# An output projection whose second half is a block of seven products, with x and x2 in quarters of the columns

## The chip, the cores and the metric

The kernel runs on one core of a Trainium2 chip. The core has five engines with a queue of instructions each: TensorE (PE in the profile) multiplies matrices into the accumulation banks (PSUM), VectorE (DVE) and ScalarE (ACT) do elementwise work, GpSimd (POOL) does a little elementwise work and issues transfers, SyncE (SP) issues transfers. They run side by side and wait for each other through semaphores. Each queue is worked in order, so an instruction that waits holds up all that is behind it on its engine.

The metric is the time of one execution on the device in microseconds, the median over the runs.

## What is computed

One layer of a decoder for 512 tokens of width 2048, in float32. What matters here is its end:

```python
        g_a, g_b = jnp.split(jax.nn.sigmoid(merge_logits), 2, axis=-1)
        merged = g_a * (o_a @ w_up_a[l]) + g_b * (o_b @ w_up_b[l])
        x = x + merged @ w_out[l]
        x = x + jax.nn.sigmoid(x @ w_ple_gate[l]) * (p[l] @ w_ple[l])
    return rms_norm(x, final_g)
```

`w_out` and `w_ple_gate` are 2048 x 2048, `merged` and `x` are 512 x 2048. The sum `x + merged @ w_out` is called x2 in the kernel. Ahead of this lie one wide input projection, attention with 16 heads and a gated mixing within chunks of 128 tokens.

## The kernel before

**Arithmetic.** Every float32 operand of the large products is split into a high part (rounded by ACT, helper `high`, line 132) and a low part (the rest, by DVE, helper `low`, line 138). A product is three matmuls: high by high, high by low, low by high. Weights come from DRAM as raw tiles and are split on the way; activations are kept split and transposed, 128 channels on the partitions and 512 tokens along the row, as 16 row tiles in four parts of four (`act_h`, `act_l`; slots h0 to h3 and l0 to l3 of one pool).

**Jobs.** All large products are `Job`s, and `gemm` (line 279) is a generator that issues their matmuls in order. The main program draws on it with `fill(n)` (n units of three matmuls or so) and `finish(name)` (up to a job's end), and puts other work between. A plain job ("N") has 512 columns; in each of its 16 steps it takes one row tile of weights and issues twelve matmuls (four token tiles, three matmuls each) into four banks. Each step first splits weights two steps ahead (`split_to`), then takes some pieces off a list of background work (`pop`; `state["pops"]` pieces in a step).

A job of kind "S" has 1024 columns as a 2 x 2 block of half the channels by half the columns, and half the tokens by half the channels on the other side. Seven products stand for eight: 28 steps of twelve matmuls instead of 32. It wants four sums of the activations (S1 to S4), made by `sum_chunk` and `s4_chunk` in the background; four differences of weights, made by DVE in `sum_to` (line 231); and at the end of the products the banks are put together by `evac_quad` (products 1, 5 and 6 are saved by ACT; 3, 7 and 2 are added to them; 4 is taken as it is). The products run in the order 1 and 5, 6 and 3, 7, 2 and 4. S1 lies in `ob_h`, S2 in `ob_l`, S4 in a tile `s4`; S3 goes out to DRAM and comes back into half of the activations' own tiles once their old values are done with. In the kernel before, the jobs vn, zb, m0 to m3, ua0 and ua1 are of this kind.

**Order.** pl (input embeddings), attention's projections and attention, u0, u1 (plain), vn, zb, m0 to m3 (seven products), ua0, ua1 (seven products), ub0 to ub3 (plain), wo0 to wo3 (plain, `w_out`), pg0 to pg3 (plain, `w_ple_gate`), and the tail with the norm and the stores. The order on each queue is written out by hand in the main program.

**Around the change.** After ub3, `turn_merged` has put the merged activations into the 16 row tiles. x is then loaded whole into the tile x2 (line 1448, four loads on POOL's queue). When a job wo ends, DVE adds its banks to x2's columns (line 667); six units later PE transposes the new quarter of x2 (line 1471, two turns of eight transposes), and ACT and DVE split it: the first half of the channels into `ob_h` and `ob_l`, the second into two more tiles, `ob2`. The gate jobs pg read those tiles. At their ends `evac_ple_gate` and `evac_last` use x2, the `ple` quarters (computed at the start and put into DRAM) and `final_g`.

Of the kernel before, what the change touches and what calls it, by code (L numbers as in the profile page):

```python
# [21 lines left out]
P = 128  # L22
# [15 lines left out]
class Job:  # L38
# [24 lines left out]
def kernel(ctx: ExitStack, tc: tile.TileContext, x, p, norm_g, w_in,  # L63
# [23 lines left out]
    small = const.tile([P, 80], F32, name="small")  # L87
# [5 lines left out]
    ph_act = ExitStack()  # L93
    edge = ctx.enter_context(tc.tile_pool(name="edge", bufs=1, side="right"))
    edge.tile([P, 56], F32, name="pad_r")
    actp = ph_act.enter_context(tc.tile_pool(name="actp", bufs=1, side="right"))
# [7 lines left out]
    for q in range(4):  # L104
        for i in "hl":
            new_part(i, q)

# [11 lines left out]
    ob_h = acts.tile([P, 8, S], F32R, name="ob_h")  # L119
    ob_l = acts.tile([P, 8, S], F32R, name="ob_l")  # L120
# [49 lines left out]
    def add_job(job):  # L170
        jobs.append(job)
        if job.kind == "S":
            half, c2 = job.kt // 2, job.c0 + job.cols
# [65 lines left out]
    def split_to(i, more=1):  # L239
        while state["high"] < len(subs):  # L240
            h = state["high"]
            job, k, n, ld = subs[h]
            if h > (i if job.kind == "S" else i + more):
                break
            sum_to(h)
            if job.kind == "S":
                hi = quad["pool"].tile([P, 2, job.cols], F32R, tag="hs", name="hs", bufs=3)
            elif k >= job.kt - job.tail:
                hi = f_tiles["th"][:, k - job.kt + job.tail:][:, :n]
            else:  # L250
                hi = stream.tile([P, n, job.cols], F32R, tag="hi", name="hi", bufs=4)
            src = source(h)
            high(hi, src)
            parts[h] = [hi, None, src]
            state["high"] += 1
        sum_to(i + 1)
        while state["low"] <= min(i, len(subs) - 1):
            job, k, n, ld = subs[state["low"]]
            pt = parts[state["low"]]
            if job.kind == "S":  # L260
                pt[1] = quad["pool"].tile([P, 2, job.cols], F32R, tag="ls", name="ls", bufs=3)
            elif k >= job.kt - job.tail:
                pt[1] = f_tiles["tl"][:, k - job.kt + job.tail:][:, :n]
            else:
                pt[1] = stream.tile([P, n, job.cols], F32R, tag="lo", name="lo")
# [186 lines left out]
    xs, ys = ("g", "g", "s", "s"), ("t", "t", "o", "o")  # L452
    vs_b, vw_b = ("t", "t", "s", "s"), ("o", "o", "t", "t")
# [84 lines left out]
    def part_act(p, k, t):  # L538
# [8 lines left out]
        o = {"5": ob_h, "6": ob_l}[p] if p in "56" else quad["s4"]  # L547
        return o[:, k, sl], o[:, k, t * P + 256:t * P + 256 + P]

    def evac_quad(final, place=None):  # L550
# [4 lines left out]
        def e(p, ps):  # L555
# [14 lines left out]
            else:  # L570
                for t in range(2):
# [3 lines left out]
                    final(2 + t, 0, stream.tile([P, 512], F32, tag="hi", name="c21", bufs=4), ps[t])  # L575
# [23 lines left out]

    ob2 = {}  # L600
# [29 lines left out]
    def load_gate_b(cg):  # L630
        up_tiles[cg] = up_tiles["pool"].tile([P, TT, 512], F32, tag="gate", name="gate", bufs=3)
        nc.gpsimd.dma_start(up_tiles[cg], gate_columns(1, cg))
# [29 lines left out]

    def evac_out(cg):
        def e(ps):
            for t in range(TT):
                sl = x2[:, t, 512 * cg:512 * cg + 512]
                nc.vector.tensor_tensor(out=sl, in0=sl, in1=ps[t], op=ALU.add)
# [5 lines left out]
    def x2_act(k):  # L673
        return ob_act(k) if k < 8 else (ob2["h"][:, k - 8], ob2["l"][:, k - 8])
# [28 lines left out]
    def evac_last(ps, t):  # L703
        ss, fg = f_tiles["ss"], f_tiles["fg"]
        if t == 0:
            f_tiles["rs"] = f_tiles["pool"].tile([P, TT, 2], F32, name="rs", bufs=1)
# [482 lines left out]
    def sum_chunk(c):  # L1189
# [16 lines left out]
        def s1():  # L1206
            op(None, l22, ALU.add)
            split(ob_h[:, k1, lo_t], ob_h[:, k1, hi_t], w["t"])

        def s2():  # L1210
            op(None, h11, ALU.subtract)
            op(None, l11, ALU.subtract)
            high(ob_l[:, k1, lo_t], w["t"])

        def s2_low():
            low(ob_l[:, k1, lo_t], ob_l[:, k1, hi_t], w["t"])
# [17 lines left out]
    def s4_chunk(c):  # L1234
# [4 lines left out]
        def first():  # L1239
            t = w["t"] = quad["pool"].tile([P, 2, 256], F32, tag="s1", name="sum", bufs=2)  # L1240
            h12, l12, h, l = (a.bitcast(F32) for a in (act_h(k2, lo_t), act_l(k2, lo_t),
                                                       ob_l[:, k1, lo_t], ob_l[:, k1, hi_t]))
# [4 lines left out]
        def second():  # L1247
            split(quad["s4"][:, k1, lo_t], quad["s4"][:, k1, hi_t], w["t"])
# [28 lines left out]
    ph_s4 = ExitStack()  # L1277
    quad["s4"] = ph_s4.enter_context(tc.tile_pool(name="s4p", bufs=1, side="right")).tile([P, 8, S], F32R, name="s4")
# [4 lines left out]
    for q in range(2):  # L1283
        for i, a in enumerate((act_h, act_l)):
            nc.gpsimd.dma_start(a(slice(4 * q, 4 * q + 4), slice(256, 512)), s3_dram[:, i, 4 * q:4 * q + 4])
# [86 lines left out]
    def load_oa(i, t):  # L1372
        t = t.rearrange("p a s -> p (a s)").rearrange("p (o h k s) -> p o h k s", h=2, k=4, s=256)
        n = t.shape[1]
        nc.gpsimd.dma_start(t, oa_dram[:, i:i + n])
        oa_slot.update((p, t[:, j]) for j, p in enumerate("1563724"[i:i + n]))

    load_oa(0, ob_h)
    fill(4 * 8)
    load_oa(2, ob_l)  # L1380
    load_oa(4, quad["s4"])
# [3 lines left out]
    ph_7 = ExitStack()  # L1385
    load_oa(6, ph_7.enter_context(tc.tile_pool(name="oa7", bufs=1)).tile([P, 4, S], F32R, name="oa7"))
# [13 lines left out]
    ph_7.close()  # L1400
    ph_q.close()
    ph_s4.close()


    obp = ctx.enter_context(tc.tile_pool(name="obp", bufs=1))
    fp = ctx.enter_context(tc.tile_pool(name="fp", bufs=1))
    f_tiles["ss"] = fp.tile([P, TT, 4], F32, name="ss")
    for i in "hl":
        ob2[i] = obp.tile([P, 8, S], F32R, name="ob2" + i)
    ph_up = ExitStack()  # L1410
    up_tiles["pool"] = ph_up.enter_context(tc.tile_pool(name="gatep", bufs=1))
# [31 lines left out]
    state["pops"] = 2  # L1443
    ph_up.close()
    mp = ctx.enter_context(tc.tile_pool(name="mp", bufs=1))
    x2 = mp.tile([P, TT, D], F32, name="x2")
    for t in range(TT):
        nc.gpsimd.dma_start(x2[:, t], x[t * P:t * P + P])


    free_banks = {0: "to", 1: "gs", 2: "to", 3: "gs"}
    for cg in range(4):
        finish(f"wo{cg}")
        if cg == 3:
            ph_act.close()
            fq = f_tiles["pool"] = ctx.enter_context(tc.tile_pool(name="fq", bufs=2))
            fg = f_tiles["fg"] = fq.tile([P, D], F32, name="fg", bufs=1)
            nc.gpsimd.dma_start(fg, bass.AP(tensor=final_g.tensor, offset=final_g.offset, ap=[[0, P], [1, D]]))
            for i in range(4):
                ple_t[i] = fq.tile([P, TT, 512], F32, tag="ple", name="ple", bufs=4)  # L1460
                nc.gpsimd.dma_start(ple_t[i], spilled(i))
            f_tiles["th"] = fq.tile([P, 8, 512], F32R, name="th", bufs=1)
            f_tiles["tl"] = fq.tile([P, 8, 512], F32R, name="tl", bufs=1)
            state["pops"] = 1
        fill(6)
        for j in (0, 2):
            pair = [bank(free_banks[cg][i], "ps_x2") for i in range(2)]
            for i, b in enumerate(pair):
                for t in range(TT):
                    k = 4 * cg + j + i  # L1470
                    nc.tensor.transpose(b[:, t * P:t * P + P], x2[:, t, k * P:k * P + P], ident)
            for i, b in enumerate(pair):
                h, l = x2_act(4 * cg + j + i)
                split(h, l, b)
            fill(8 if cg < 3 else 16)
# [26 lines left out]
```

## Time and profile before

| | |
|---|---|
| median of 3 runs | 1585.43 us |
| lowest and highest | 1585.24 and 1585.61 us |
| profiled execution | 1584.71 us |
| its span, first to last instruction | 1583.0 us |
| mean granted clock of TensorE | 0.999 |

The span is what the profile's views divide up; the profiled execution's time has 1.7 us around it. In the page, a line such as `L138 DVE ... lo<-raw,hi` is a group of instructions: line of the kernel, engine, operation, tile written from tiles read, sizes, count, busy time in all and mean of one, then the idle time of the engine just before them and what ended it. Matmuls overlap on TensorE, so that their mean durations add up to more than the time that passes.

### The profile page before, as it was taken

To read this page: it belongs to the slowest core of one execution; us is meant where nothing else is said; L and a number is where in the kernel's file an instruction comes from. 1 tells how busy PE (TensorE), PEld (TensorE's weight loads), DVE (VectorE), ACT (ScalarE), POOL (GpSimd) and SP (SyncE) were. 2 spreads that over 40 slices of the span, in tenths; PEclk is the share of its full clock that TensorE was granted. 3 is DMA by queue.
4 is the path that set the end of the run, shared out by engine and by line. 5 is a ranking of instruction groups with operands and counts; after the bars stand their busy time and mean duration, and the time that the engine had idled before them with its cause. 6 is when DMAs were issued, how large, how long until landed. Compare 5 with 4: busy or idle time off the path is not lost.

```text
span 1583.0 us, 20477 instructions
## 1 busy us (share of the span) xinstructions
PE 1569.2 (99%) x7582; PEld 1314.1 (83%) x7582; DVE 1038.4 (66%) x1717; ACT 723.7 (46%) x1289; POOL 209.1 (13%) x315
## 2 busy tenths in 40 slices
PE   9999999999999999999999999999999999999997
PEld 8889988888888888888888888888888888888886
DVE  6543358889887797878978777777566333333335
ACT  7433346667664444455544454454232222223334
POOL 1200000110113420001112112110123000001101
PEclk9999999999999999999999999999999999999999
DMA  9432432121215992536555556873732533363333
GB/s 330 120 81 76 112 81 54 41 54 41 54 49 144 260 305 77 189 97 209 180 201 180 191 162 209 292 282 138 252 114 87 201 92 93 93 226 97 104 94 133
DMA packets 144132, 229.38 MB, mean 145 GB/s; under 512 B 7816, under 2 KB 74016, under 8 KB 141728
## 3 DMA queue, kind: packets, MB, share of 16 engines
q1 hardware_dynamic: 114768, 150.00, 31.0%
q0 software_dynamic: 29120, 77.71, 14.3%
q8 instruction: 59, 0.97, 0.3%
q14 instruction: 41, 0.34, 0.1%
q10 hardware_dynamic: 144, 0.36, 0.1%
HBM read 188.72 MB, written 39.32 MB: 144 GB/s over the span
## 4 chain that ended last, share of the span: by engine, by line
PE 97%; DVE 2%; ACT 1%; issue 0%; POOL 0%; DVEq 0%; POOLq 0%; ACTq 0%
PE ps_m L302 6%; PE ps_m L304 6%; PE ps_m L303 6%; PE ps_wo L342 4%; PE ps_wo L340 4%; PE ps_wo L341 4%; PE ps_pg L342 3%; PE ps_pg L341 3%; PE ps_pg L340 3%; PE ps_t L1007 2%; PE ps_za L328 2%; PE ps_za L330 2%; PE ps_za L329 2%; PE ps_u L340 2%; PE ps_ub L340 2%; PE ps_u L341 2%
## 5 line engine op out<-in xcount | busy, mean ns | idle before, releaser
L138 DVE TENSOR_TENSOR lo<-raw,hi 128x512 fp32r<-128x512 f32 (+1 forms) x312 | 217.2, 701 | 268.9 <-PE ps_pg L341 84.1
L132 ACT CAST hi<-raw 128x512 fp32r<-128x512 f32 (+1 forms) x312 | 189.4, 612 | 354.3 <-PE ps_wo L342 110.1
L138 DVE TENSOR_TENSOR ls<-b,hs 128x1024 fp32r<-128x1024 f32 x140 | 171.3, 1224 | 96.5 <-ACT hs L132 95.9
L132 ACT CAST hs<-b 128x1024 fp32r<-128x1024 f32 x140 | 147.2, 1052 | 166.6 <-PE ps_m L304 86.6
L302 PE MATMUL ps_m<-hs,act_h 128*128 128x512 f32 x256 | 100.5, 393 | 0.0
L340 PE MATMUL ps_wo<-hi,act_h 128*128 128x512 f32 x256 | 100.3, 392 | 0.0
L303 PE MATMUL ps_m<-ls,act_h 128*128 128x512 f32 x256 | 99.7, 389 | 0.0
L342 PE MATMUL ps_wo<-hi,act_l 128*128 128x512 f32 x256 | 99.7, 389 | 0.0
L341 PE MATMUL ps_wo<-lo,act_h 128*128 128x512 f32 x256 | 99.7, 389 | 0.0
L304 PE MATMUL ps_m<-hs,act_l 128*128 128x512 f32 x256 | 99.7, 389 | 0.0
L132 ACT CAST hs<-raw 128x1024 fp32r<-128x1024 f32 x56 | 59.0, 1053 | 74.8 <-PE ps_m L304 35.2
L132 ACT CAST pth<-ps_t 128x512 fp32r<-128x512 f32 (+1 forms) x88 | 47.9, 544 | 65.7 <-PE ps_t L1007 65.4
L138 DVE TENSOR_TENSOR ls<-raw,hs 128x1024 fp32r<-128x1024 f32 x56 | 68.4, 1222 | 13.1 <-ACT hs L132 13.0
L968 ACT ACTIVATE prob<-prob,st 128x512 f32<-128x512 f32 (+3 forms) x128 | 70.7, 555 | 4.0 <-DVE st L959 3.8
L138 DVE TENSOR_TENSOR ptl<-ps_t,pth 128x512 fp32r<-128x512 f32 (+1 forms) x88 | 56.1, 638 | 21.1 <-ACT pth L132 20.3
L231 DVE TENSOR_TENSOR b<-b,b 128x1024 f32<-128x1024 f32 x56 | 68.2, 1217 | 0.0
L231 DVE TENSOR_TENSOR b<-raw,b 128x1024 f32<-128x1024 f32 x56 | 68.2, 1217 | 0.0
L959 DVE CUSTOM_DVE_ANT_0 prob<-ps_s,b 128x512 f32<-128x512 f32 (+3 forms) x128 | 56.3, 485 | 10.1 <-PE ps_s L956 9.8
L304 PEld LDWEIGHTS ps_m<-hs,act_l 128*128 128x128 f32 x256 | 48.1, 188 | 10.1
L342 PEld LDWEIGHTS ps_wo<-hi,act_l 128*128 128x128 f32 x256 | 48.0, 188 | 10.1
L341 PEld LDWEIGHTS ps_wo<-lo,act_h 128*128 128x128 f32 x256 | 48.1, 188 | 9.8
L302 PEld LDWEIGHTS ps_m<-hs,act_h 128*128 128x128 f32 x256 | 48.1, 188 | 9.7
(452 smaller groups left out, 4160.2 us busy)
## 6 DMA issues: line engine op xcount, KB each, us to landing
raw<-in_w_in_dram SPq DMA_DIRECT2D x116, 512.0 KB, 3.8
b<-in_w_in_dram SPq DMA_DIRECT2D x48, 512.0 KB, 5.4
raw<-in_w_out_dram SPq DMA_DIRECT2D x32, 512.0 KB, 3.6
raw<-in_w_ple_gate_dram SPq DMA_DIRECT2D x32, 512.0 KB, 3.6
raw<-in_w_up_b_dram SPq DMA_DIRECT2D x16, 512.0 KB, 3.9
oa_d<-oa POOLq DMA_DIRECT2D x28, 256.0 KB, 3.8
gate<-keep POOLq DMA_DIRECT2D x24, 256.0 KB, 3.8
xt<-in_x_dram SPq DMA_DIRECT2D x4, 1024.0 KB, 9.6
```

Of the source, the lines that this page charges most:

```text
L132: nc.scalar.copy(hi, src)
L138: nc.vector.tensor_tensor(out=lo, in0=src, in1=hi.bitcast(F32), op=ALU.subtract)
L231: nc.vector.tensor_tensor(out=b[o], in0=b[x], in1=b[y], op=ALU.subtract)
L302: nc.tensor.matmul(o, ah, hi[:, i], start=st, stop=False, skip_group_check=go)
L303: nc.tensor.matmul(o, ah, lo[:, i], start=False, stop=False, skip_group_check=go)
L304: nc.tensor.matmul(o, al, hi[:, i], start=False, stop=sp, skip_group_check=go)
L328: nc.tensor.matmul(ps, hi[:, j], ah, start=st, stop=False)
L340: nc.tensor.matmul(o, ah[:, sl], hi[:, j], start=st, stop=False)
L341: nc.tensor.matmul(o, ah[:, sl], lo[:, j], start=False, stop=False)
L342: nc.tensor.matmul(o, al[:, sl], hi[:, j], start=False, stop=sp)
L959: nc.vector.tensor_tensor_reduce(out=pt[:, j * n:j * n + n], in0=o[:, j], in1=b0[:, 512 - n:], scale=-SLOPE[h], scalar=3.0e38, op0=ALU.add ...
L968: nc.scalar.activation(sl, sl, AF.Exp, bias=st[:, 0, j, hh:hh + 1], scale=-1.0, accum_out=st[:, 1, j, hh:hh + 1])
```

## The change

The jobs wo2 and wo3 (columns 1024 to 2047 of `w_out`) become one job of kind "S", `wo2`, with the halves of its columns exchanged: `c0` is 1536, and a new argument `c2` gives 1024. The sums it wants are made in the background of wo0 and wo1, from the merged activations.

It needs `ob_h`, `ob_l` and the `s4` tiles for S1, S2 and S4, and the pool of the block jobs stays open. So there is no room for the whole of x2 and for `ob2`. x is loaded a quarter of the columns at a time into a tile `x` (the last quarter into the first `s4` tile). Each quarter, when its columns of the product have been added, is stored to DRAM (`x2_dram`), transposed, and split: quarter 0 through a staging tile into DRAM (`x2t_dram`), to be loaded into the slots h0 and l0 when product 7 has ended; quarter 1 into `ob_h` after product 5; quarter 2 into `ob_l` after product 6; quarter 3 into the slots h1 and l1. In the gate stage x2 is loaded again, a quarter for each job, and so are the `ple` quarters, into the slots h2, h3, l2, l3. The gate jobs take their banks in turn from two sets, and the second half of the last job's kept weights lies in the `s4` tiles.

```diff
-    def __init__(self, name, kind, w, c0, cols, kt, act, evac, banks=None, tail=0):
+    def __init__(self, name, kind, w, c0, cols, kt, act, evac, banks=None, tail=0, c2=None):
...
+        self.c2 = c0 + cols if c2 is None else c2
...
+    sums_of = {"5": [ob_h[:, 4 * q:4 * q + 4] for q in range(2)], "6": [ob_l[:, 4 * q:4 * q + 4] for q in range(2)],
+               "3": [None, None]}
...
-    def evac_quad(final, place=None):
+    def evac_quad(final, place=None, tiles=True):
...
-        up_tiles[cg] = up_tiles["pool"].tile([P, TT, 512], F32, tag="gate", name="gate", bufs=3)
+        up_tiles[cg] = new_s4(cg - 1, F32) if cg in (1, 2) else new_x()
...
+    x_tiles = {}
+    x2_dram = dram.tile([S, D], F32, name="x2_d")
+    x2t_dram = dram.tile([P, 2, 4, S], F32R, name="x2t_d")
+
+    def add_x(cg, t, src):
+        nc.vector.tensor_tensor(out=x_tiles[cg][:, t], in0=x_tiles[cg][:, t], in1=src, op=ALU.add)
...
-    for cg in range(4):
-        add_job(Job(f"wo{cg}", "N", w_out, 512 * cg, 512, KT, h_act, evac_out(cg), (ys, xs)[cg % 2]))
...
+    for cg in range(2):
+        add_job(Job(f"wo{cg}", "N", w_out, 512 * cg, 512, KT, h_act, evac_out(cg), (ys, xs)[cg]))
+    add_job(Job("wo2", "S", w_out, 1536, 512, KT, part_act,
+                evac_quad(lambda t, c, o, src: add_x(2 if c else 3, t, src), tiles=False), ("o", "t", "s"), c2=1024))
...
-        add_job(Job(f"pg{cg}", "N", w_ple_gate, 512 * cg, 512, KT, x2_act,
-                    evac_ple_gate(cg) if cg < 3 else evac_last, ys, tail=0 if cg < 3 else 8))
+        add_job(Job(f"pg{cg}", "N", w_ple_gate, 512 * cg, 512, KT, h_act,
+                    evac_ple_gate(cg) if cg < 3 else evac_last, (zs, os_)[cg % 2], tail=0 if cg < 3 else 8))
...
+    sums_of["3"] = [new_s4(q) for q in range(2)]
+    for f in (sum_chunk, s4_chunk):
+        for c in range(4):
+            background.extend(f(c))
+    state["pops"] = 1.4
...
+    def turn_x2(cg, banks, dest, n):
         for j in (0, 2):
-            pair = [bank(free_banks[cg][i], "ps_x2") for i in range(2)]
+            pair = [bank(banks[i], "ps_x2") for i in range(2)]
...
+                dest(j + i, b)
+            fill(n)
+
+    def stage(k, b):
+        o = quad["pool"].tile([P, 2, S], F32R, tag="hs", name="x2t", bufs=3)
+        split(o[:, 0], o[:, 1], b)
+        nc.gpsimd.dma_start(x2t_dram[:, :, k], o)
+
+    load_x(0, new_x())
+    finish("wo0")
+    store_x2(0)
+    fill(6)
+    turn_x2(0, "to", stage, 8)
+    load_x(1, new_x())
+    finish("wo1")
+    assert not background
+    store_x2(1)
+    load_s3()
+    fill(4 * 8)
+    turn_x2(1, "gg", lambda k, b: split(ob_h[:, k], ob_h[:, 4 + k], b), 4)
+    load_x(2, new_x())
+    fill(4 * 6)
+    load_x(3, new_s4(0, F32))
+    fill(4 * 6)
+    store_x2(2)
+    x2_parts = {i: {0: new_part(i, 0)} for i in "hl"}
+    for n, i in enumerate("hl"):
+        nc.gpsimd.dma_start(x2_parts[i][0], x2t_dram[:, n])
+    turn_x2(2, "gg", lambda k, b: split(ob_l[:, k], ob_l[:, 4 + k], b), 4)
+    finish("wo2")
...
+    load_ple(0)
+    fill(10)
+    store_x2(3)
+    turn_x2(3, "os", lambda k, b: split(act_h(12 + k), act_l(12 + k), b), 8)
...
+    load_x2(0)
+    state["pops"] = 1
+    for cg in range(3):
+        finish(f"pg{cg}")
+        load_ple(cg + 1)
+        load_x2(cg + 1)
     finish("pg3")
```

`load_x`, `store_x2`, `load_x2` and `load_ple` are single transfers on POOL's queue.

More of the change, by code (lines that the diff above doesn't have):

```diff
@@ L86 @@
     warm = const.tile([P, 1], F32, name="warm")
-    small = const.tile([P, 80], F32, name="small")
+    small = const.tile([P, 104], F32, name="small")
     bst = small[:, 0:48].rearrange("p (t c i) -> p t c i", t=TT, c=2)
@@ L172, in add_job @@
         if job.kind == "S":
-            half, c2 = job.kt // 2, job.c0 + job.cols
+            half, c2 = job.kt // 2, job.c2
             ld = {}
@@ L248, in split_to @@
             elif k >= job.kt - job.tail:
-                hi = f_tiles["th"][:, k - job.kt + job.tail:][:, :n]
+                hi = f_tiles["tail"]("h", k - job.kt + job.tail)
             else:
@@ L262, in split_to @@
             elif k >= job.kt - job.tail:
-                pt[1] = f_tiles["tl"][:, k - job.kt + job.tail:][:, :n]
+                pt[1] = f_tiles["tail"]("l", k - job.kt + job.tail)
             else:
@@ L574, in e @@
                         continue
-                    final(2 + t, 0, stream.tile([P, 512], F32, tag="hi", name="c21", bufs=4), ps[t])
+                    final(2 + t, 0, stream.tile([P, 512], F32, tag="hi", name="c21", bufs=4) if tiles else None, ps[t])
         return e
@@ L705, in evac_last @@
         if t == 0:
-            f_tiles["rs"] = f_tiles["pool"].tile([P, TT, 2], F32, name="rs", bufs=1)
+            f_tiles["rs"] = small[:, 96:104].rearrange("p (t c) -> p t c", t=TT)
         r = f_tiles["rs"]
@@ L1282, with load_s3 @@
     finish("u1")
-    for q in range(2):
-        for i, a in enumerate((act_h, act_l)):
-            nc.gpsimd.dma_start(a(slice(4 * q, 4 * q + 4), slice(256, 512)), s3_dram[:, i, 4 * q:4 * q + 4])
+    def load_s3():
+        for q in range(2):
+            for i, a in enumerate((act_h, act_l)):
+                nc.gpsimd.dma_start(a(slice(4 * q, 4 * q + 4), slice(256, 512)), s3_dram[:, i, 4 * q:4 * q + 4])
+    load_s3()
     finish("zb")
@@ L1372, in load_oa @@
     def load_oa(i, t):
[L1373 to L1378, printed above, removed]
+        t = t.rearrange("p a s -> p (a s)").rearrange("p (h k s) -> p h k s", h=2, k=4)
+        nc.gpsimd.dma_start(t, oa_dram[:, i])
+        oa_slot["1563724"[i]] = t
+    for i in range(2):
+        load_oa(i, ob_h[:, 4 * i:4 * i + 4])
     fill(4 * 8)
-    load_oa(2, ob_l)
-    load_oa(4, quad["s4"])
+    for i in range(2):
+        load_oa(2 + i, ob_l[:, 4 * i:4 * i + 4])
+    for i in range(2):
+        load_oa(4 + i, new_s4(i))
     finish("m3")
@@ L1442 @@
             load_gate_b(3)
[L1443 to L1465, printed above, removed]
+    sums_of["3"] = [new_s4(q) for q in range(2)]
@@ new lines, with load_x2 @@
+    th = fq.tile([P, 8, 512], F32R, name="th")
+    tl = [new_s4(q) for q in range(2)]
+    f_tiles["tail"] = lambda i, k: th[:, k:k + 1] if i == "h" else tl[k // 4][:, k % 4:k % 4 + 1]
+    f_tiles["ss"] = small[:, 80:96].rearrange("p (t c) -> p t c", t=TT)
+    nc.gpsimd.dma_start(fg, bass.AP(tensor=final_g.tensor, offset=final_g.offset, ap=[[0, P], [1, D]]))
+    def load_x2(cg):
+        nc.gpsimd.dma_start(x2[:, :, 512 * cg:512 * cg + 512], columns(x2_dram, cg))
+    load_x2(0)
+    state["pops"] = 1
```

81 lines of the change are left out of this document (46 added, 35 removed).

## The prediction

> **What bounds the kernel now.** I read the page's first part, the chain of waits, the table of waits of TensorE, a table of stretches cut at the stages, and then groups of instructions inside single stages.
>
> ```profile
> PE 1569.2 (99%) x7582; PEld 1314.1 (83%) x7582; DVE 1038.4 (66%) x1717; ACT 723.7 (46%) x1289; POOL 209.1 (13%) x315
> ...
> PE 97%; DVE 2%; ACT 1%; issue 0%; POOL 0%; DVEq 0%; POOLq 0%; ACTq 0%
> ```
>
> TensorE (PE) works 99% of the span and makes 97% of the chain that ended last. So an instruction taken from PE shortens the kernel, as long as nothing makes PE wait afterwards. Whether anything does now is in the table of PE's waits, whole but for its heading:
>
> ```profile
> PE ps_spin L768 <- POOL eps_t L85: 1.4, 1, 1.4
> PE ps_t L1007 <- DVE ptl L138: 1.3, 1, 1.3
> PE ps_pl L336 <- ACT hi L132: 0.8, 1, 0.8
> PE ps_s L955 <- ACT pct L1100: 0.2, 1, 0.2
> ```
>
> Four short waits, none behind the attention stage. Now the stages, in columns of length, then busy time of PE, its weight loads, VectorE (DVE), ScalarE (ACT), GpSimd (POOL), granted clock, DMA share, GB/s:
>
> ```profile
> 490.50:578.90 88.40, 88.40 (x394) 72.89 (x393) 74.25 (x126) 40.14 (x71) 31.14 (x46) 1.00 0.95 273
> 655.10:731.20 76.10, 76.10 (x337) 63.05 (x336) 60.00 (x58) 36.86 (x43) 4.30 (x8) 1.00 0.42 138
> 1215.90:1397.20 181.30, 181.30 (x834) 150.78 (x833) 65.31 (x97) 48.45 (x80) 7.08 (x8) 1.00 0.37 116
> 1397.20:1573.50 176.30, 176.27 (x785) 145.62 (x783) 73.15 (x114) 64.63 (x121) 19.90 (x17) 1.00 0.39 128
> ```
>
> They are u0 and u1; zb; the four output projections wo0 to wo3; the gate projections pg0 to pg3. PE is full in all, at full clock; behind them lies a tail of 9.5 us. The second row matters most: zb is a block of seven products over 1024 columns and 16 row tiles of weights, what the change makes of wo2 and wo3.
>
> **The price of a step.** A matmul is shown with 389 to 393 ns, but matmuls overlap, so that number must not be used. A plain job has 16 steps of twelve matmuls (a quarter-step, below, is three), and DVE's low part of a weight tile waits for PE once in a step, so the distance of two such rows is a step:
>
> ```profile
> 1234.06 0.69 DVE L138 TENSOR_TENSOR lo<-raw,hi 128x512 fp32r<-128x512 f32 x1 [2.03 <-PE ps_wo L341]
> ...
> 1258.54 0.69 DVE L138 TENSOR_TENSOR lo<-raw,hi 128x512 fp32r<-128x512 f32 x1 [2.03 <-PE ps_wo L341]
> 1259.44 2.67 DVE L667 TENSOR_TENSOR x<-x,ps_wo 128x512 f32<-128x512 f32 x4 [0.21 <-PE ps_wo L342]
> ...
> 1265.32 1.03 PE L1471 MATMUL ps_x<-ident,x 128*128 128x128 f32 x8
> ```
>
> The last two rows are DVE's adds of x at wo0's end and the first turn behind it (eight transposes, 1.03 us). Nine steps lie between the first two rows: 24.48/9 = 2.72 us. Two plain jobs, 32 steps, take 87.0 us without transposes. The seven products of zb, 28 steps, took 76.1 us (28 x 2.72 = 76.2).
>
> **Removed: four steps of PE.** 87.0 - 76.1 = 10.9 us. The transposes of x2 stay 16 tiles in eight turns, so they cancel. If nothing waits, this is the whole result. Everything else in the change is off PE and costs nothing where it is covered. None of it can come out below nothing: the stages show PE without a wait that could go. So I go through the covers in the order of time.
>
> **Added in wo0 and wo1: sums of the merged activations.** The seven products need four sums (S1 to S4), made by sum_chunk and s4_chunk as for vn and zb. Per chunk they are 11 and 4 DVE operations (with the low parts), four chunks: 60.
>
> ```profile
> L1198 DVE TENSOR_TENSOR sum<-sum,act_l 128x512 f32<-128x512 f32 x20 | 13.8, 688 | 0.4
> ...
> L138 DVE TENSOR_TENSOR lo<-raw,hi 128x512 fp32r<-128x512 f32 x64 | 45.1, 705 | 98.9 <-PE ps_wo L341 82.8 <-issue 16.1
> L132 ACT CAST hi<-raw 128x512 fp32r<-128x512 f32 x64 | 39.9, 624 | 122.0 <-PE ps_wo L342 110.1 <-DVE x L667 6.3 <-DMA raw<-in_w_out_dram 3.6
> ...
> 565.00:578.90 13.90, 13.90 (x63) 11.49 (x62) 13.47 (x20) 6.17 (x10) 1.01 (x3) 1.00 1.06 382
> ```
>
> 60 x 0.688 = 41.3 us on DVE. When they are queued, 22 quarter-steps of wo0 are issued; 10 steps of wo0 and 16 of wo1 remain, at 1.4 pieces a step 36.4, and the pieces are 4 x (7 + 2) = 36. In these 26 steps (70.7 us of PE, about 73 with two turns) DVE has the sums, 26 low parts of 0.705 (18.3), four adds of x (2.67) and the four low parts of the turned x2 (2.8 by the same row): 65 us, 89%. The last row above, from the end of u1 where the same sums run, has DVE at 97% and PE at 13.90 of 13.90 us. Cost: nothing. If that cover is gone, DVE is late by what it has over 73 us, which from 65 needs 8 us more.
>
> At wo0's end DVE's adds must end before the turn six quarter-steps later. In the old trace they end at 1259.44 + 2.67 = 1262.1, and the turn's matmuls begin at 1265.3: 3.2 us of room. The longest piece ahead of the adds (s1: add, wait for ACT's high part, low part) is about 2.0 us by the rows of 0.69 and 0.62, and a low part 0.7: 2.7 us, inside the room. Bounds 0 and 1 us; I take 0, nearest the rows.
>
> **wo2, seven products over 1024 columns.** zb is its model: weights, differences of weights, rings and saved banks are the same code. zb's groups:
>
> ```profile
> L138 DVE TENSOR_TENSOR ls<-b,hs 128x1024 fp32r<-128x1024 f32 x20 | 24.5, 1223 | 14.1 <-ACT hs L132 14.0
> L132 ACT CAST hs<-b 128x1024 fp32r<-128x1024 f32 x20 | 21.0, 1052 | 24.6 <-PE ps_zb L304 22.4 <-DVE b L231 2.0 <-ACT hs L132 0.2
> ...
> L591 DVE SCALAR_TENSOR_TENSOR keep<-g,keep 128x512 f32<-128x512 f32 x4 | 2.6, 683 | 0.0
> ```
>
> DVE waits for ACT, and ACT waits for PE (22.4 us): both run ahead of PE and are stopped by the buffers. Of zb's 60.0 us on DVE, 2.6 are its own ends (last row); wo2 has eight adds of x in their place (8 x 0.67 = 5.3) and eight low parts of turned x2 (8 x 0.705 = 5.6): 68.3 us in 76.1 + 2 = 78 us, 88%, where u0 and u1 have 84% (74.25 of 88.40) and u1's end 97% with PE full. Cost: nothing; the upper bound is that the added 8.3 us come out whole on PE.
>
> The two turns inside wo2 have only the two "g" banks: the second half of a turn may not begin until both banks of the first are split. Four quarter-steps (2.72 us) lie between. By the row of 0.62, ACT has two saved banks from the products before and then two high parts, and DVE's second low part ends the split: 4 x 0.62 + 0.7 = 3.2 us from the end of those products. The second half is reached after the first's transposes and the four quarter-steps, 1.0 + 2.7 = 3.7 us. Half a microsecond of room is little with DVE 88% busy, so a small wait is likely once. Bounds 0 and 1.5 us; I take 0.4, nearer the row's end.
>
> x's third quarter is loaded into the tile that x2's second quarter leaves: after its store and its transposes, 9 steps into wo2. Behind the wait, on POOL's queue, stand only the fourth quarter's load and later stores. It is used 8 steps (22 us) later by DVE's add.
>
> **Queues.** SP's queue gets wo2's weights in the form of zb's: two rings of four and the raw ring, 8 MB as before, started in the middle of wo1 as vn's were in u1. POOL's queue gets the most: x still comes in four loads; added are four stores and four loads of x2 (8 MB), four stores and two loads of the transposed quarter (4 MB), eight stores and four loads of S3 (4 MB). That is 16 MB and 26 issues of at most 0.78 us (rows below), 20 us of POOL in some 350, and 46 GB/s beside the 116 and 128 of the stages; at u1's end the DMA share was 1.06 with PE full. POOL's own adds in ub3 come before all of it, its multiplications by final_g behind the loads that are issued when a gate job ends: both have tens of microseconds.
>
> **The way by DRAM, up to pg0.** pg0 starts with the first quarter of x2 transposed, put into DRAM during wo1 and read back into the slots h0 and l0, free after product 7. The two loads of 1 MB are issued behind the store of x2's third quarter, 22 of wo2's 28 steps in. Cover: 6 x 2.72 + 2 = 18 us. No row shows exactly this; the nearest are groups of 1 MB transfers on POOL's queue issued at once:
>
> ```profile
> 1124.18 2.25 POOL L632 DMA_DIRECT2D gate<-gate  x3 [15.27 <-PE ps_ua L304]
> ...
> DMA to landing us min/median/max: 5.6/8.2/12.4
> ...
> L1461 POOL DMA_DIRECT2D ple<-spill x4: 748/756/763, 1398.2 to 1400.4; - x4
> ...
> DMA to landing us min/median/max: 9.2/13.5/17.4
> ```
>
> Three loads together (and a fourth later) landed within 12.4 us of their issue, four behind a fifth within 17.4. Three transfers of 3 MB in all are the first case: landing 6 us before pg0. Cost nothing, by the nearest row. The upper bound is one transfer after another, each at the slowest of the first group: 3 x 12.4 = 37.2 us, 19.2 too late.
>
> A rule of the Trainium skill speaks against this place: in "SBUF — State Buffer", section "SBUF: two separate sides", GpSimd's port is locked out while DVE holds it in some of its operations, and DMAs of the POOL queue then wait for their descriptors. By that rule the loads would come late just because DVE is 88% busy, and the sum would go to the upper bound, which is rival 2. The rows bear it out little:
>
> ```profile
> L1285 POOL DMA_DIRECT2D act_h<-s_d x2: 768/769/770, 580.8 to 582.3; - x2
> ...
> DMA to landing us min/median/max: 5.9/7.1/9.4
> ```
>
> Four loads of 0.5 MB, issued within 2.2 us with DVE still busy from u1's end, landed within 9.4 us.
>
> **ub0 to ub3.** The gates' second half now lies in the x and s4 tiles. The old loads waited for ua1's last product (15.27 us in the row of three above) and the new ones do too, with ub0's 8 steps, 21.8 us, ahead of the first use: nothing.
>
> **pg0 to pg3.** Same matmuls from other tiles; the two sets of banks save nothing, for PE waited for none. x2 and the ple quarters now come a quarter at a time, a job (43.5 us) ahead of use, against 17.4 us for the slowest landing: nothing. The tail is the same code.
>
> **Sum.** The profiled execution is 1584.71 us: span 1583.0 and 1.7 around it. 1584.7 - 10.9 + 0.4 = 1574.2. The median of the runs is 0.7 above the profiled execution, so I forecast 1574.9 us.
>
> **Rivals.**
> (1) DVE becomes the bound in wo2. For it: 88 to 89% busy and in order. Against: u1's end at 97% without a wait. Priced whole: 8.3 us lost, -10.5 + 8.3 = -2.2, 1583.2 us; if it is lost in part, between this and the forecast.
> (2) Slower than before: pg0 waits for its first quarter. Place: the end of wo2; nothing else can run on PE then, so lateness is paid one for one. It decides from a landing 18 + 10.5 = 28.5 us after issue; at the upper bound of 37.2 us the kernel loses 19.2 - 10.5 = 8.7: 1594.1 us. For it: three transfers in a row and loads of weights beside them. Against: 12.4 and 17.4 above.
> (3) The sums run, but x's third quarter lands late and holds up DVE: a wait of DVE behind POOL. Issue at step 9, use at step 17: 22 us against 17.4 at worst; if it came 5 us late, two steps of lookahead hide it. Net -10.5 up to about -8, 1577.4 us.
>
> **Chances.** Forecast 0.66; rival 3 or other small waits, up to 4 us, 0.09; rival 1 at 0.12; rival 2 at 0.10; something unseen 0.03. Forecast and small waits lie between 1573.0 (a little under the bare -10.9, for the spread of the profiled execution) and 1578.9, rival 1 up to 1583.2, so the range 1573.0 to 1583.2 leaves out rival 2 and the unseen. What can be told from no change is 0.2%, 3.2 us: from 1582.3 on, which is the upper end of rival 1, two thirds of it being faster. Faster 0.66 + 0.09 + 0.08 = 0.83; same 0.04 + 0.01 = 0.05; slower 0.10 + 0.02 = 0.12.
>
> **What would show it.** PE should have 48 matmuls fewer, wo0's first to pg0's first some 170.8 us instead of 181.3, and the table of PE's waits no new row over 1 us. A wait of a pg0 matmul for a DMA shows rival 2; one for the weight tiles hs or ls in wo2, with DVE near 100%, rival 1; DVE's add of x2 waiting for a load, rival 3. The prediction is wrong if the stage shrinks by 10.9 and another grows, or if the step in wo2 is not 2.72 us.

## The result and the profile after

The changed kernel takes **1601.98 us** (median of 4 runs, 1601.96 to 1603.66) against 1585.52 us of the kernel before beside it: ratio **1.0106, 95% interval 1.0089 to 1.0124**, slower by 16.5 us. The forecast was 1574.9 us. The profiled execution took 1601.99 us with a span of 1600.3 us.

From the page of the changed kernel, the busy time of the engines and the engines' shares of the chain that ended last:

```profile
PE 1585.2 (99%) x7534; PEld 1306.4 (82%) x7534; DVE 1109.7 (69%) x1795; ACT 745.2 (47%) x1307; POOL 230.2 (14%) x344
...
PE 96%; DVE 2%; ACT 1%; issue 0%; DVEq 0%; POOL 0%; POOLq 0%; ACTq 0%
```

PE has 48 matmuls fewer (7534 for 7582), as the change says, and is busy 16 us longer (1585.2 for 1569.2). So the loss is hardly made of waits. The table of PE's waits in the changed kernel, whole but for its heading:

```profile
PE ps_wo L312 <- DVE ls L147: 1.8, 1, 1.8
PE ps_spin L780 <- POOL eps_t L86: 1.4, 1, 1.4
PE ps_t L1019 <- DVE ptl L147: 1.2, 1, 1.2
PE ps_pl L345 <- ACT hi L141: 0.6, 1, 0.6
PE ps_s L967 <- ACT pct L1112: 0.2, 1, 0.2
```

One wait is new, 1.8 us in wo2. It can't be the 16 us. The stages show where they are; the table of stretches of the changed kernel, columns as in the prediction, for u0 and u1, zb, m0 to m3, ub0 to ub3, wo0 and wo1, wo2, and the gate jobs:

```profile
495.50:586.30 90.80, 90.80 (x395) 72.90 (x394) 75.71 (x126) 41.08 (x71) 31.74 (x47) 1.00 0.93 267
664.40:742.40 78.00, 78.00 (x337) 63.03 (x336) 59.95 (x58) 36.77 (x43) 4.31 (x8) 1.00 0.42 134
742.40:1065.60 323.20, 323.20 (x1441) 262.51 (x1441) 252.79 (x250) 154.24 (x180) 62.46 (x106) 1.00 0.59 195
1142.70:1235.10 92.40, 92.40 (x433) 77.03 (x432) 54.98 (x73) 26.68 (x46) 21.82 (x17) 1.00 0.42 138
1235.10:1328.30 93.20, 93.20 (x418) 75.44 (x418) 68.84 (x104) 33.23 (x54) 15.77 (x19) 1.00 0.67 213
1328.30:1411.90 83.60, 81.84 (x370) 66.30 (x369) 65.68 (x70) 37.01 (x45) 7.90 (x11) 1.00 0.53 164
1411.90:1590.80 178.90, 178.90 (x785) 145.59 (x783) 74.39 (x116) 63.94 (x120) 22.81 (x21) 1.00 0.45 150
```

The reader is to see that u0 begins at 495.5 us instead of 490.5 and wo0 at 1235.1 instead of 1215.9. **The kernel is 19.2 us late before the first instruction of the changed job.** u0 and u1 have the same matmuls as before (395 for 394 in the records), the same clock and DVE load, no wait, and take 90.8 us for 88.4; zb takes 78.0 for 76.1. m0 to m3 take 323.2 for 316.1. But ub0 to ub3 take 92.4 us in both kernels. The rows of the kernel before for m0 to m3 and for ub0 to ub3:

```profile
731.20:1047.30 316.10, 316.09 (x1441) 262.52 (x1440) 252.37 (x250) 154.49 (x180) 60.86 (x103) 1.00 0.59 200
...
1123.50:1215.90 92.40, 92.40 (x433) 77.02 (x432) 54.98 (x73) 26.69 (x46) 21.86 (x17) 1.00 0.43 138
```

The changed stages do gain: wo0's first matmul to pg0's first is 176.8 us for 181.3, though only 4.5 of the 10.5 us forecast. The gate jobs lose 2.6 us (178.9 for 176.3).

Next to each other on PE, in the kernel before and in the changed one, six matmuls apart (columns: start, duration, instruction):

```profile
1240.15 0.39 PE L340 MATMUL ps_wo<-hi,act_h 128*128 128x512 f32 x1
...
1241.51 0.39 PE L340 MATMUL ps_wo<-hi,act_h 128*128 128x512 f32 x1
```

```profile
1260.24 0.39 PE L350 MATMUL ps_wo<-lo,act_h 128*128 128x512 f32 x1
...
1261.64 0.39 PE L350 MATMUL ps_wo<-lo,act_h 128*128 128x512 f32 x1
```

Six matmuls take 1.36 us in the one (0.2267 each) and 1.40 us in the other (0.2333), with the duration shown unchanged at 0.39. A plain step of twelve is then 2.80 us instead of 2.72. In ub0 to ub3 of the changed kernel the old distance holds:

```profile
1179.83 0.39 PE L349 MATMUL ps_ub<-hi,ob_h 128*128 128x512 f32 x1
...
1181.19 0.39 PE L349 MATMUL ps_ub<-hi,ob_h 128*128 128x512 f32 x1
```

These are 1.36 us for six again. The same instruction on the same shape has two prices in one kernel, and the rows that matter differ only in the operand from the activations, `act_h` or `ob_h`. A slice of it, 128x128, is what a weight load (LDWEIGHTS) brings in for the next matmul; the other operand, 512 columns of `hi` or `lo`, is the one streamed against it. One weight load of the changed kernel, beside the matmul that starts at 1260.24 above:

```profile
1260.24 0.19 PEld L351 LDWEIGHTS ps_wo<-hi,act_l 128*128 128x128 f32 x1
```

Tiles lie in SBUF in two groups. Those of the weights (raw, hi, lo, hs, ls) and `ob_h`, `ob_l` grow from the left edge; `act_h`, `act_l` and the s4 tiles grow from the right. In the changed kernel two small sums of the norm (`ss`, `rs`) moved into the constants' tile, by a line of the change that the prediction gave no price:

```diff
-    small = const.tile([P, 80], F32, name="small")
+    small = const.tile([P, 104], F32, name="small")
```

It adds 24 words of 4 bytes, 96 bytes, in each partition. Every tile to the left of the gap moves by 96 bytes, none on the right does. The tiles named here begin, group by group, at the same place within blocks of 512 bytes: left at 0 and right at 256 in the kernel before, left at 96 and right at 256 in the changed one. Below, "distance" is the difference of these two: 256 before, 160 after, 0 for two operands of one group. It is read from where the tiles lie in the compiled kernels.

### The profile page after: what moved, and what is told of

Its sections match the earlier page's. It is cut to its first block, busy times and chain, and to the rows that moved or that the text cites. A ratio compares the mean times of both kernels' runs of the same rounds, so it can differ in the third digit from the quotient of the medians.

```text
span 1600.3 us, 20479 instructions
## 1 busy us (share of the span) xinstructions
PE 1585.2 (99%) x7534; PEld 1306.4 (82%) x7534; DVE 1109.7 (69%) x1795; ACT 745.2 (47%) x1307; POOL 230.2 (14%) x344
## 4 chain that ended last, share of the span: by engine, by line
PE 96%; DVE 2%; ACT 1%; issue 0%; DVEq 0%; POOL 0%; POOLq 0%; ACTq 0%
PE ps_m L312 7%; PE ps_m L311 7%; PE ps_m L313 6%; PE ps_pg L350 3%; PE ps_pg L349 3%; PE ps_pg L351 3%; PE ps_t L1019 2%; PE ps_u L351 2%; PE ps_za L337 2%; PE ps_za L338 2%; PE ps_u L350 2%; PE ps_u L349 2%; PE ps_za L339 2%; PE ps_ub L351 2%; PE ps_ub L349 2%; PE ps_ub L350 2%
## 5 line engine op out<-in xcount | busy, mean ns | idle before, releaser
L147 DVE TENSOR_TENSOR lo<-raw,hi 128x512 fp32r<-128x512 f32 (+1 forms) x280 | 195.0, 702 | 186.6 <-PE ps_pg L350 85.4
L141 ACT CAST hi<-raw 128x512 fp32r<-128x512 f32 (+1 forms) x280 | 169.2, 609 | 284.7 <-PE ps_pg L351 97.4
L147 DVE TENSOR_TENSOR ls<-b,hs 128x1024 fp32r<-128x1024 f32 x160 | 195.9, 1224 | 116.2 <-ACT hs L141 115.3
L141 ACT CAST hs<-b 128x1024 fp32r<-128x1024 f32 x160 | 167.8, 1050 | 198.2 <-PE ps_m L313 87.6
L147 DVE TENSOR_TENSOR ls<-raw,hs 128x1024 fp32r<-128x1024 f32 x64 | 78.3, 1223 | 16.5 <-ACT hs L141 16.5
L311 PEld LDWEIGHTS ps_m<-hs,act_h 128*128 128x128 f32 x256 | 48.1, 188 | 11.6
L312 PEld LDWEIGHTS ps_m<-ls,act_h 128*128 128x128 f32 x256 | 48.1, 188 | 11.1
L337 PE MATMUL ps_za<-act_h,hi 128*128 128x512 f32 x128 | 55.9, 437 | 0.0
L337 PE MATMUL ps_q<-act_h,hi 128*128 128x512 f32 x128 | 54.0, 422 | 0.0
L1019 PEld LDWEIGHTS ps_t<-ident,prob 128*128 128x128 f32 x320 | 39.8, 140 | 14.0 <-DVE ptl L147 2.8
L351 PE MATMUL ps_wo<-hi,act_l 128*128 128x512 f32 x128 | 51.0, 398 | 0.0
```

What stands on the lines that cost most here:

```text
L141: nc.scalar.copy(hi, src)
L147: nc.vector.tensor_tensor(out=lo, in0=src, in1=hi.bitcast(F32), op=ALU.subtract)
L311: nc.tensor.matmul(o, ah, hi[:, i], start=st, stop=False, skip_group_check=go)
L312: nc.tensor.matmul(o, ah, lo[:, i], start=False, stop=False, skip_group_check=go)
L337: nc.tensor.matmul(ps, hi[:, j], ah, start=st, stop=False)
L351: nc.tensor.matmul(o, al[:, sl], hi[:, j], start=False, stop=sp)
```

## The experiments

The theories that the runs had to tell apart: the time is lost by the addresses (the 96 bytes), whatever the change does; or by the changed work (DVE's sums, the transfers, the wait in wo2). Later runs ask by what rule of addresses, and what the wait in wo2 costs. Letters and forms in the quoted expectations are those of the text they stand in.

**1. The changed kernel, distance put back to 256.** An unused filler tile stands at the right edge; making it 96 bytes smaller moves the right group by the 96 bytes too, and no instruction changes.

```diff
-    edge.tile([P, 56], F32, name="pad_r")
+    edge.tile([P, 32], F32, name="pad_r")
```

> The changed kernel with the filler at the right end of the memory cut from 56 to 32 words, so that all tiles of the right side (activations, s4) move up by 96 bytes as the larger tile small moved those of the left side (weights, ob, the block pool). Theory A, the distance between the two sides sets the pitch of matmuls that read one operand from each: pitch back from 0.233 to 0.227 us, wo0's first matmul to pg0's first about 172 us, 1574 to 1577 us. Theory B, the start of the left side alone (96 bytes into a block of 512) is what slows: still 1602 us. Theory C, the seven products, the way by DRAM or the queues cost the time: still 1602 us.

Measured: 1577.03 us (1576.12 to 1577.78), ratio to the kernel before 0.9945 (0.9928 to 0.9962). The changed kernel loses 25.0 us and beats the old one by 8.5 when nothing but the addresses is put back. Stretches of this run, for u0 and u1, zb, wo0 and wo1, wo2, the gate jobs:

```profile
490.80:579.20 88.40, 88.40 (x395) 72.89 (x394) 74.25 (x126) 40.15 (x71) 31.15 (x46) 1.00 0.96 273
655.30:731.40 76.10, 76.10 (x337) 63.00 (x337) 60.09 (x58) 36.86 (x43) 4.31 (x8) 1.00 0.43 138
1216.10:1306.80 90.70, 90.70 (x418) 75.41 (x417) 68.47 (x104) 33.30 (x54) 15.74 (x19) 1.00 0.69 218
1306.80:1390.60 83.80, 81.60 (x369) 67.40 (x368) 65.90 (x70) 37.06 (x45) 7.90 (x11) 0.98 0.52 164
1390.60:1566.60 176.00, 176.00 (x785) 145.61 (x783) 73.92 (x115) 64.01 (x120) 22.75 (x21) 1.00 0.46 152
```

u0 and u1, and zb, have their old lengths to the tenth, wo0 begins at 1216.1 (1215.9 before), the gate jobs are back at 176.0. Only wo2 is still too long, so that wo0's first matmul to pg0's first takes 174.5 us, where theory A said about 172.

**2. The kernel before, with the distance of the changed one.** Only `small` grows from 80 to 104 words, the line of the change shown above and nothing else of it.

> The kernel before with one number changed: the tile small has 104 words instead of 80; nothing reads the added words. Theory A: the left side moves by 96 bytes against the right side, as in the changed kernel; u0 and u1 take 90.8 us instead of 88.4, zb 78.0 instead of 76.1, the whole about 1585.5 + 28 = 1613 us (more than the changed kernel's loss, because four plain jobs wo are slowed). Theory B: the same. Theory C: 1585.5 us.

Measured: 1609.12 us (1609.09 to 1609.64), ratio 1.0150 (1.0135 to 1.0165): 23.6 us lost by 24 words that nothing uses. Its stretches, for u0 and u1, zb, ub0 to ub3, and wo0 to wo3:

```profile
495.40:586.30 90.90, 90.90 (x395) 72.95 (x395) 75.67 (x126) 41.10 (x71) 31.78 (x47) 1.00 0.94 266
664.30:742.30 78.00, 78.00 (x337) 62.98 (x337) 60.03 (x58) 36.78 (x43) 4.31 (x8) 1.00 0.41 135
1142.70:1235.20 92.50, 92.50 (x434) 77.05 (x433) 55.13 (x73) 26.70 (x46) 22.00 (x17) 1.00 0.43 138
1235.20:1421.50 186.30, 186.30 (x834) 150.79 (x832) 65.25 (x97) 48.30 (x80) 7.01 (x8) 1.00 0.36 113
```

The stages of the changed kernel are there without the change: wo0 begins at 1235.2, and ub keeps its length. u0 and u1, and zb, came as expected; the whole was put 4 us too high (1613).

**3. Other distances in the kernel before.** The same line with 96, 88, 112 and 128 words, to see which rule the distance follows.

```diff
-    small = const.tile([P, 80], F32, name="small")
+    small = const.tile([P, 96], F32, name="small")
```

> The kernel before with small at 96 words: the left side moves by 64 bytes. Theory A in the form that only the distance by 64 bytes counts (160 bytes of distance is no multiple of 64, 256 and 192 are): 1585.5 us. Theory A in the form that 256 bytes in 512 are needed: slower, between 1590 and 1613 us. Theory C: 1585.5 us.

> The kernel before with small at 88 words: the left side moves by 32 bytes, and the two sides are 224 bytes apart (in 512) instead of 256. Form 1 (the farther from 256, the slower; 192 cost 8.6 us and 160 cost 23.6): about 1588 us. Form 2 (odd multiples of 32 are slow, multiples of 64 less, multiples of 128 fast): about 1609 us.

> The kernel before with small at 112 words: 128 bytes apart. Form 1: 1609 us or more. Form 2: 1585.5 us.

> The kernel before with small at 128 words: 64 bytes apart. Form 1: 1609 us or more, unless the cost falls again towards a distance of 0. Form 2: 1594 us, as with 192 bytes.

**4. Start or distance.** The left group begins at 96 as in experiment 2, but the filler shrinks by 96 bytes too, so that the distance is 256 again:

```diff
-    small = const.tile([P, 80], F32, name="small")
+    small = const.tile([P, 104], F32, name="small")
...
-    edge.tile([P, 56], F32, name="pad_r")
+    edge.tile([P, 32], F32, name="pad_r")
```

> The kernel before with small at 104 words and the filler at 32: both sides are moved by 96 bytes, their distance stays 256. Theory A (the distance): 1585.4 us. Theory B (where the left side starts): 1609 us, as e2.

And distance 0: both groups begin at 480.

```diff
-    small = const.tile([P, 80], F32, name="small")
+    small = const.tile([P, 72], F32, name="small")
...
-    edge.tile([P, 56], F32, name="pad_r")
```

> The kernel before with small at 72 words and no filler: both sides begin at 480 in a block of 512, a distance of 0. If what counts is that operands lie a multiple of 256 bytes apart, as with ub0 to ub3, whose operands lie on one side and which kept their 92.2 us in every run: 1585.5 us. If the 256 were a lucky value of its own: slower, 1594 to 1609 us.

All of them are the kernel before, with these two tiles changed; the last column is against the kernel before in the same comparison.

| left, right, distance (bytes) | median | runs | against before |
|---|---|---|---|
| 96, 352, 256 | 1585.14 us | 10 | -0.3 us, ratio 0.9999 (0.9989 to 1.0008) |
| 480, 480, 0 | 1585.85 us | 8 | +0.4 us, ratio 1.0003 (0.9993 to 1.0013) |
| 32, 256, 224 | 1604.92 us | 1 | +19.7 us |
| 64, 256, 192 | 1594.05 us | 2 | +8.6 us, ratio 1.0054 (1.0034 to 1.0074) |
| 96, 256, 160 | 1609.12 us | 4 | +23.6 us, ratio 1.0150 (1.0135 to 1.0165) |
| 128, 256, 128 | 1604.24 us | 1 | +19.0 us |
| 192, 256, 64 | 1603.25 us | 1 | +18.0 us |

The rows at 96 settle that the start of a tile alone does nothing: the left group at 96 is fast with the right one at 352 and slow with it at 256. Distances 0 and 256 are fast, the five in between are slow, 192 less than its neighbours. The traces show it in the pitch too: in wo0 to wo3, from one matmul's start to the next, 0.227 us on average at 0 and 256, 0.229 at 192, and 0.232 to 0.234 at the other four, three of which rest on one run each. Of the two forms named for 96 words, the one by multiples of 64 fails (192 costs 8.6 us) and the one that wants 256 fits. The two forms put forward for 88, 112 and 128 words don't give these values (1588 or 1609 us for 1604.92, 1609 or 1585.5 for 1604.24, 1609 or 1594 for 1603.25), and none that I have does.

**5. The wait in wo2.** In experiment 1, wo2 takes 83.8 us instead of some 80. The new wait and the matmuls around it, on PE:

```profile
1312.21 0.39 PE L311 MATMUL ps_wo<-hs,act_h 128*128 128x512 f32 x1
1314.80 0.80 PE L312 MATMUL ps_wo<-ls,act_h 128*128 128x512 f32 x1 [2.20 <-DVE ls L147]
1315.40 0.63 PE L313 MATMUL ps_wo<-hs,act_l 128*128 128x512 f32 x1
...
1317.96 0.45 PE L313 MATMUL ps_wo<-hs,act_l 128*128 128x512 f32 x1
```

and on DVE in the same run:

```profile
1308.02 0.69 DVE L1257 TENSOR_TENSOR sum<-sum,act_l 128x512 f32<-128x512 f32 x1
1309.40 0.69 DVE L147 TENSOR_TENSOR s<-sum,s 128x512 fp32r<-128x512 f32 x1 [0.69 <-ACT s L141]
1310.01 2.47 DVE L675 TENSOR_TENSOR x<-x,ps_wo 128x512 f32<-128x512 f32 x4
1312.40 1.21 DVE L240 TENSOR_TENSOR b<-b,b 128x1024 f32<-128x1024 f32 x1
1313.54 2.49 DVE L147 TENSOR_TENSOR ls<-b,hs 128x1024 fp32r<-128x1024 f32 x2
```

wo2 begins at 1306.8. DVE is then still at the last piece of S4, its low part waits 0.69 us for ACT, wo1's four adds of x (2.47) stand behind it, then a difference of weights, and only then the two low parts that the third step needs: PE stands still for 2.2 us. Afterwards six matmuls take 2.56 us (1315.40 to 1317.96), 0.427 each instead of 0.227. The granted clock in stretches of 2 us of that run:

```profile
1314.00:1316.00 2.00, 1.20 (x3) 1.00 (x4) 1.95 (x3) 1.71 (x2) 2.00 (x4) 0.66 0.96 356
1316.00:1318.00 2.00, 2.00 (x7) 1.52 (x6) 2.00 (x3) 0.00 (x0) 0.53 (x1) 0.50 0.95 211
```

It is 0.66 and 0.50: by an estimate from these two, about 1.7 us more (2 x 0.34 + 2 x 0.50). So in this execution a wait of 2.2 us costs some 3.9. It is the slowest of four (1577.78 us, against 1576.12 for the fastest), so the others lost less. If the last pieces of S4 are issued a little sooner, DVE is free ahead of wo2, and the wait should go. The next run is experiment 1 with more pieces a step:

```diff
-    state["pops"] = 1.4
+    state["pops"] = 1.6
```

> e1 with 1.6 instead of 1.4 pieces of the sums taken in a step, so that the 36 pieces end some 3.5 steps before wo1 does. Theory D, PE's wait of 2.2 us in wo2's third step and the lower clock behind it come from DVE having the last sums and x's adds before the weights' difference and low part: the wait goes, wo2 takes about 79.5 us instead of 83.8, the whole 1572.5 to 1574 us. Theory E, the wait is for late weights or is inherent in going from a plain job to a block: the wait stays, 1577 us.

Measured: 1573.94 us (1573.55 to 1574.52), ratio 0.9929 (0.9915 to 0.9943), 3.1 us under experiment 1. Its stretches for wo0 and wo1, wo2, and the gate jobs, with DVE at the start of wo2:

```profile
1216.40:1307.00 90.60, 90.60 (x417) 75.36 (x416) 72.81 (x110) 33.57 (x56) 15.71 (x19) 1.00 0.69 218
1307.00:1386.80 79.80, 79.80 (x369) 66.38 (x368) 61.99 (x64) 35.62 (x43) 7.88 (x11) 1.00 0.56 172
1386.80:1562.90 176.10, 176.07 (x785) 145.61 (x783) 74.04 (x115) 63.99 (x120) 22.59 (x21) 1.00 0.46 152
```

```profile
1303.07 2.43 DVE L147 TENSOR_TENSOR ls<-b,hs 128x1024 fp32r<-128x1024 f32 x2
1305.41 2.51 DVE L675 TENSOR_TENSOR x<-x,ps_wo 128x512 f32<-128x512 f32 x4
```

The low parts now stand ahead of the adds, PE has no wait in wo2, and some 4 us of DVE's work have moved out of wo2's stretch (61.99 for 65.90) into the one before (72.81 for 68.47). wo2 is 79.8 us for 83.8.

**6. A version without a moved tile.** Instead of the smaller filler, `small` stays at 80 words and the sums of the norm use 24 words of the filler tile, which nothing else uses; pieces as in experiment 5.

```diff
-    small = const.tile([P, 104], F32, name="small")
+    small = const.tile([P, 80], F32, name="small")
...
-    edge.tile([P, 56], F32, name="pad_r")
+    spare = edge.tile([P, 56], F32, name="pad_r")
...
-            f_tiles["rs"] = small[:, 96:104].rearrange("p (t c) -> p t c", t=TT)
+            f_tiles["rs"] = spare[:, 16:24].rearrange("p (t c) -> p t c", t=TT)
...
-    state["pops"] = 1.4
+    state["pops"] = 1.6
...
-    f_tiles["ss"] = small[:, 80:96].rearrange("p (t c) -> p t c", t=TT)
+    f_tiles["ss"] = spare[:, 0:16].rearrange("p (t c) -> p t c", t=TT)
```

> The changed kernel with the filler back at 56 words and small back at 80, the 24 added words taken from the filler tile itself, and 1.6 pieces in a step: nothing moves against the kernel before. Theory A: as e5, 1573 to 1575 us. If the 24 words cost something as such, above 1575.

Measured: **1573.83 us** (1573.65 to 1573.98), ratio 0.9927 (0.9915 to 0.9940), as experiment 5. It is faster than both kernels: with nothing moved and the last pieces issued sooner, the change is worth 11.6 us.

## Why the prediction was wrong

The account in medians: the change with the old distance and DVE in time gains 11.3 us (experiment 5); the wait in wo2 takes back 3.1 (experiment 1 less 5); the distance takes back 25.0 (the changed kernel less experiment 1). -11.3 + 3.1 + 25.0 is +16.8, against 16.5 measured. The split between the last two is rough: the wait was 1.8 us at full clock in the changed kernel's profile, 2.2 us with a lower clock behind it in experiment 1's.

**The failed step: "Everything else in the change is off PE and costs nothing where it is covered", with the price of a step taken over as 2.72 us.** The prediction went through work and waits and gave every moved tile the price of its transfers. It left out that a tile of constants grew, since no instruction comes of it. Its own last condition, that it is wrong "if the step in wo2 is not 2.72 us", is what happened: the step is 2.80 us, and in u0, zb and m0 to m3 as well as in wo2. The bound "none of it can come out below nothing" held; there was no such care for the other side. No rival had this mechanism: the case was in the 0.03 for something unseen. That experiments 5 and 6 end within 1.1 us of the forecast is no credit to it as it stood: their addresses are back where the prediction took them to be, and their last pieces are issued sooner.

**Removed, 10.9 us: right.** With the old distance and no wait, wo0's first to pg0's first is 1386.8 - 1216.4 = 170.4 us, 10.9 under 181.3; the forecast was 170.8.

**Sums in wo0 and wo1 at no cost: right for these two jobs, wrong at their end.** wo0 and wo1 take 90.7 us in experiment 1 with DVE 75% busy, without a wait. But the 36 pieces were counted into room for 36.4, as a sum over the 26 steps, and the last pieces are issued in the last steps; they end at 1310.1, 3.3 us into wo2. What is late next was not asked: the adds of x behind the pieces, then the weights' low parts behind the adds.

**wo2's DVE at no cost (rival 1 otherwise): in between.** A wait for `ls` is the sign that the prediction gave for rival 1. It costs 3.1 us of the 8.3, and it comes from the order at one place, not from DVE as the bound: DVE's load in wo2 is 65.90 of 83.80 us, under the 68.3 forecast, and with the pieces issued sooner the wait is gone. A share of busy time could not show it. The 78 us by which the prediction divided that load are too few: the two quarters turned within wo2 have four sets of eight transposes, 4.1 us and not 2, which makes 80.2 us and 85% instead of 88%; experiment 5 took 79.8.

**The "g" turns, 0.4 us: not seen.** No run has a row for it among PE's waits.

**The way by DRAM (rival 2) and x's third quarter (rival 3): nothing, as forecast.** The two loads of the transposed quarter, and x's loads, in the changed kernel (columns: shortest, median and longest issue in ns, first and last start), each group with its times from issue to landing:

```profile
L1515 POOL DMA_DIRECT2D act_h<-x2t_d x1: 567/567/567, 1393.2 to 1393.2; - x1
L1515 POOL DMA_DIRECT2D act_l<-x2t_d x1: 582/582/582, 1393.7 to 1393.7; - x1
...
DMA to landing us min/median/max: 9.4/10.5/11.7
...
L1475 POOL DMA_DIRECT2D x<-in_x_dram x3: 758/766/787, 1248.8 to 1358.6; - x3
...
DMA to landing us min/median/max: 5.7/6.6/7.4
```

At most 11.7 us from an issue at 1393.7 is 1405.4, 6.5 us ahead of pg0's first matmul at 1411.9; the estimate was 12.4 and 6. They were in time with DVE 79% busy in wo2 (65.68 of 83.60 us). The prediction took the rule in "SBUF: two separate sides" of the Trainium skill's page "SBUF — State Buffer" to make them late just because DVE is busy. The section says less: it ties the lockout to DVE operations in a two-port mode, or with two SBUF inputs against a GpSimd operation that reads SBUF, and not to DVE's share of busy time. No run here shows which of wo2's operations would be of these, so the landings neither bear the rule out nor speak against it.

**The gate jobs: wrong in the changed kernel by 2.6 us, for the first reason.** The kernel before reads `ob_h`, `ob_l` and `ob2` there, where ub shows the short pitch with `ob_h`. The change puts half of x2 into `act` slots, the right group. With the distance at 256 the stage is 176.0 us, as before.

## What to carry to other kernels

A change of a tile's size is a change of every address behind it: when a kernel becomes slower from its first stage on, in stages that were not touched, compare the pitch of the same instruction in both traces, and put the addresses back alone before looking at the changed work. When background work is planned by a sum over steps, ask where its last piece falls, and what stands behind it on the same engine when the next job starts. A change whose measured total is a loss may still hold its gain: here 11.6 us (with DVE's last pieces in time), under a loss of some 25 that one line brought.

## What was not expected of the hardware

**The pitch of matmuls depends on where the two operands lie to each other.** At full granted clock it is 0.227 us at distances 0 and 256 and 0.233 at 160, for the same 128x512 matmul; over the kernel before that is up to 23.6 us of 1585. The section "Step-by-step: what each phase is for" of the page "TensorE: Matmul & The Clock Gate" in the Trainium skill says that PE reads the streamed operand and the next weights through two independent ports, so that loading weights takes no bandwidth from the running matmul. By that rule the distance would do nothing, and the runs differ from it.

That the two reads meet in the memory is only a guess, and the places where neighbouring matmuls change sides don't settle it. In the jobs of seven products, with the streamed operand on the left, the time from a matmul's start to the next one's can be read where the loaded operand goes from left to right and where it goes back. At distance 224 it is 235 ns on the way to the right and 227 on the way back, at 160 it is 237 and 229, as if the operand loaded for the next matmul counted; but at 64 it is the other way round, 226 and 230. Nor does the distance give every interval: in m0 to m3 of the changed kernel, matmuls that read `ob_h` or `ob_l`, in groups of twelve or so between others, follow each other in 229.6 ns on average against 227.1 in the kernel before, with both operands on the left. Other distances were not tried; whether 512 bytes is the true period, and why 192 costs 8.6 us and 224 costs 19.7, stays open.

**A lower clock followed a wait of 2.2 us.** In experiment 1 the granted clock fell to 0.50 behind it; in the changed kernel, behind a wait of 1.8 us at the same place, it stayed at 1.00:

```profile
1334.00:1336.00 2.00, 0.24 (x2) 0.05 (x1) 1.95 (x3) 1.13 (x2) 2.00 (x3) 1.00 0.37 145
1336.00:1338.00 2.00, 2.00 (x9) 1.63 (x10) 2.00 (x2) 0.87 (x1) 1.67 (x3) 1.00 1.02 322
```

The section "What's actually happening" of the same page of the Trainium skill gives a free-running window of about 3.4 us, at least one of them idle, before the clock is halved; 2.2 us is less than that. One case of each is too little to say where the limit lies, and the kernel alone may not decide it: the changed kernel's four runs took 1601.96 to 1601.99 us three times and 1603.66 once, the last at a mean clock of 0.997 where the others have 0.998 and 0.999.
